# A diffusion step on one core: the order of the modulation's matmuls, the place of two half norms, and the engine of one subtraction

## The chip, the cores and the metric

The kernel runs on one core of a Trainium2 chip. The metric is the device time of one execution in microseconds (us). The core's engines work side by side, each through its own queue in order: TensorE (PE, with PEld for its weight loads), VectorE (DVE), ScalarE (ACT), GpSimd (POOL) and SyncE (SP), which issues most of the DMAs.

## The reference

The reference is one step of a diffusion model with two layers, on 128 context tokens and 512 latent tokens of width 1024 in fp32. Layer 0 mixes the tokens by grouped-query attention (8 query heads, 2 key heads), layer 1 by a gated DeltaNet (8 heads, forward and backward scan). Cut to the part that the change touches:

```python
def modulation(cond, w_mod, b_mod):              # cond: c for latent, c_ctx for context tokens
    m = jax.nn.silu(cond) @ w_mod + b_mod        # (1024) @ (1024, 6 * 1024), once per layer
    return jnp.split(m[..., None, :], N_MOD, axis=-1)

def trunk_layer(x, mods, gain1, gain2, w1, w2, mixer):
    shift1, scale1, gate1, shift2, scale2, gate2 = mods
    mix, aux = mixer(rms_norm(x, gain1) * (1 + scale1) + shift1)
    x = x + gate1 * mix
    h = rms_norm(x, gain2) * (1 + scale2) + shift2
    x = x + gate2 * (jnp.square(jax.nn.relu(h @ w1)) @ w2)     # w1: 1024 x 4096
    return x, aux

def delta_mixer(...):
    ...                                          # projections, convolution, chunked scan per head
    o = rms_norm(o, norm_gain) * silu(z)         # per head of 128
    return o.reshape(B, T, DN_VAL) @ w_out, states
```

After both layers a final RMS norm gives the output.

## The kernel before

**Layout.** Activations lie transposed: 128 features on the partitions, 640 tokens along the row, eight such tiles for the width of 1024. The tokens are worked on in two halves of 320. A product of fp32 precision is made of three matmuls on values split into a high and a low part (high by high, high by low, low by high; `mm3`, line 173 is the matmul). A half tile, that is 128 output features for 320 tokens, takes 24 matmuls of this kind.

**Dense products.** `dense` walks the columns of a weight matrix 128 at a time. `pair` loads the 1024x128 weights into one of three buffers with the tag "raw" (on SP's queue), ScalarE copies the high part, and VectorE, or the engine given as `eng`, subtracts to get the low part (`split`, line 160). Line 160 is also every other elementwise operation of two tensors, line 163 every ScalarE activation, lines 166 and 170 the operations with a scalar on VectorE. In the last product before a norm, five tiles form a group (`last=GROUP`): all their first halves come first, then `mid()` runs the norm of the first half, then the second halves follow. `prefetch` prepares three pairs ahead in six buffers with the tag "wpair".

**Norms.** While a residual is added, `norm_acc` squares each feature tile on ScalarE and adds the squares up on GpSimd. `mod_norm` sums the columns with matmuls of one column (line 289, into "nps"), takes the root on VectorE and PE, and writes the eight modulated tiles, the odd ones with GpSimd's help. It is called once for each half.

**Modulation.** The product with `w_mod` is made in three slabs of 2048 columns for each layer. A slab has eight k-steps, and each of these four matmuls, one for each group of 512 columns. The four write to different 32-row stripes of one PSUM tile, with the conditioning vector, padded to 32 columns, as the stationary operand (line 408). The slabs are fed in different ways. Slab (0, 0) is at the start of the kernel, from buffers of its own. Slab (0, 1) stands beside the key and value projections, and (0, 2) beside the attention's output product, both from two "raw" buffers for each step. Slab (1, 0) stands in the MLP of layer 0, from two "wpair" buffers for each step, tiles named "wm". Slabs (1, 1) and (1, 2) stand in the last three rounds of the DeltaNet, six steps in each, from one "raw" buffer and two activation buffers, fetched one step ahead.

**What sets the order.** Each engine's queue is ordered ahead of time by a planner, which goes by the order in which the program was traced and by when it reckons each instruction to be ready. `weave` traces several pieces of work in turns, by given shares. `pinned` does the same for a main piece and a side piece, and ties each instruction of the side piece on PE, VectorE and ScalarE behind the newest main instruction of the same engine, with an edge that sets order only and no semaphore. In the MLP of layer 0 the main piece has 128 steps (half tiles), and the side piece is slab (1, 0) followed by `presplit`, 58 steps that split the DeltaNet's weights and write them back to memory; the rate is 74 side steps on 128. Near the 123rd half tile `mid2` fetches the first DeltaNet weights and makes the norm of the first half.

**The DeltaNet.** Round r traces the projections of head r, the decay of head r-1, the inverse of head r-2 and the scan of head r-3 together (`delta`). Each scan begins with two loads of a state (line 1151). The rounds 8 to 10 have no projections of heads left; they carry the gates z (`gated`) and slabs (1, 1) and (1, 2). Behind the last round stands `dn_out` of head 7, with norm operations of 128x5, transposes (line 176) and the final scale. `out_begin` makes the first three output tiles, `dense` with `eng=nc.gpsimd` the other five.

Of the kernel before, what the change touches and what calls it, by code (L numbers as in the profile page):

```python
# [37 lines left out]
GROUP = 5  # L38
# [39 lines left out]
def weave(*parts):  # L78
    live = [[0, n, i, g] for i, (g, n) in enumerate(parts)]
    while live:  # L80
        live.sort(key=lambda e: ((e[0] + 1) / e[1], e[2]))
        e = live[0]
        try:
            next(e[3])
            e[0] += 1
        except StopIteration:
            live.pop(0)


PINNED = tuple(getattr(mybir.EngineType, n) for n in ("PE", "DVE", "Activation"))  # L90


def pinned(tc, main, n, side, m):
    nc = tc.nc
    last = {}
    why = mybir.DependencyInfo(mybir.DependencyClass.NoSync, mybir.DependencyReason.DATA)
    traced = lambda i: nc.cur_bb.bb.instructions[i:]
    at = len(traced(0))
    done = step = 0
    for _ in main:  # L100
        step += 1
        for i in traced(at):
            if i.engine in PINNED:
                last[i.engine] = i.name
        at = len(traced(0))
        while done * n < step * m and next(side, True) is None:
            done += 1
            for i in traced(at):
                if i.engine in last:
                    tc.add_manual_dep(i, last[i.engine], why, reason="paced")  # L110
            at = len(traced(0))
    drain(side)


def drain(g):
    for _ in g:
        pass


class Model:  # L120
# [277 lines left out]
    def modulate(self, l, slab, fetch, alloc=None, early=False):  # L398
        nc = self.nc
        acc = alloc or (lambda: self.ps("mod", 1))  # L400
        ps = acc()[:, :512]
        get = lambda k: fetch(self.a["w_mod"][l, k * P : (k + 1) * P, slab * 2048 : (slab + 1) * 2048])
        ahead = get(0) if early else None
        for k in range(FT):
            views = ahead or get(k)
            ahead = get(k + 1) if early and k + 1 < FT else None
            for q in range(4):
                nc.tensor.matmul(  # L408
                    ps[32 * q : 32 * q + 32, :], self.cond[:, k, :], views[q],
                    start=k == 0, stop=k == FT - 1, tile_position=(0, 32 * q),  # L410
                )
            yield
        yield from self.modulation(l, slab, ps, acc)

# [343 lines left out]
    def psum(self, name):  # L758
        return self.tc.tile_pool(name=name, bufs=1, space=bass.MemoryType.PSUM)
# [559 lines left out]
    def run(self):  # L1319
        tc, nc, a = self.tc, self.nc, self.a  # L1320
        pool = lambda name: tc.tile_pool(name=name, bufs=1)
        psum = self.psum
        FC = [f * P for f in range(FT)]
        with pool("start") as self.ph, psum("ps0") as self.pq:
            xs = self.load_x()
            self.setup()
            x = self.transpose_x(xs)
            r0 = self.token_rstd(xs)
            self.columns()
            tail = lambda: max(i for i, t in enumerate(nc.cur_bb.bb.instructions) if t.engine == PINNED[0])  # L1330
            traced = nc.cur_bb.bb.instructions
            after = traced[tail()]
            gm = self.modulate(0, 0, self.fetch_start)
            with tc.issue_after(after):
                for _ in range(FT):
                    next(gm)
            self.key_weights()
            h = self.first_norm(x, r0, gm)
            self.q0 = self.pair(a["attn_w_in"][0], 0, 0)
        with pool("attn") as self.ph:  # L1340
            self.attention(h, x)
            first = self.prefetch(a["attn_w_out"][0], 0, FC)
        with pool("mlp0") as self.ph, psum("ps3") as self.pq:
            self.extra = 3
            x = self.reload(self.xd)
            h = self.new_h()
            nxt = []

            def mid():
                nxt[:] = self.prefetch(a["mlp_w1"][0], 0, FC)  # L1350
                self.mod_norm(x, 0, 1, h, 0)

            weave((self.modulate(0, 2, self.fetch_raw), 18),
                  (self.dense(a["attn_w_out"][0], 0, FC, self.att, self.residual(x, 0, 2), first=first, last=GROUP, mid=mid), 16))
            self.mod_norm(x, 0, 1, h, 1)
            h2 = self.new_h()
            nxt2 = []

            def mid2():
                w = a["dn_w_in"][0]  # L1360
                nxt2[:] = [self.pair(w, 0, kind * D) for kind in (1, 0, 2)]
                self.mod_norm(x, 1, 0, h2, 0)

            def beside():
                yield from self.modulate(1, 0, self.fetch_pairs, early=True)
                yield from self.presplit()

            pinned(tc, self.mlp(0, h, x, nxt, mid2), 128, beside(), 74)
            self.mod_norm(x, 1, 0, h2, 1)
            h = h2  # L1370
            xd = self.spill(x, nc.scalar)
        with pool("delta") as self.ph, psum("ps4") as self.pq:
            self.extra = 0
            self.delta(h, nxt2)
            x = self.reload(xd)
            self.out_begin(x)
        with pool("mlp1") as self.ph, psum("ps5") as self.pq:
            self.extra = 4
            acts = [self.acts[i] for i in range(HEADS)]
            for half in range(2):  # L1380
                for o in range(len(self.first)):
                    self.norm_acc(x, o, half)
            h = self.new_h()
            nxt3 = []

            def mid3():
                nxt3[:] = self.prefetch(a["mlp_w1"][1], 0, FC)
                self.mod_norm(x, 1, 1, h, 0)

            done = len(self.first)  # L1390
            sink = self.residual(x, 1, 2)
            drain(self.dense(a["dn_w_out"][0], 0, FC[done:], acts, lambda o, half, ps: sink(o + done, half, ps), last=GROUP, mid=mid3, eng=nc.gpsimd))
            self.mod_norm(x, 1, 1, h, 1)
            fn = a["final_norm"]
            gain = self.wp.tile([P, D], F32, tag="wpair", bufs=self.NW, name="fgain")
            nc.scalar.dma_start(out=gain, in_=bass.AP(fn.tensor, fn.offset, [[0, P], [1, D]]))

            def final(half):
                cols = self.ps("nps", 2)
                if half == 0:  # L1400
                    blocks = (0, 1)
                    for i, b in enumerate(blocks):
                        self.rstd_cols(cols, i, [(0, P, 0, b * P)])
                else:
                    blocks = (2, 3, 4)
                    self.rstd_cols(cols, 0, [(0, P // 2, 0, 2 * P)])
                    self.rstd_cols(cols, 0, [(P // 2, P // 2, 1, 0)])
                    for i in (1, 2):
                        self.rstd_cols(cols, i, [(0, P, 1, (i + 2) * P - HALF)])
                r = self.finish_rstd(cols[:, : len(blocks)])  # L1410
                for i, b in enumerate(blocks):
                    y = self.wp.tile([P, D], F32, tag="wpair", bufs=self.NW, name=self.nm("y"))
                    for c in range(0, D, 512):
                        ps = self.dense_ps()
                        for j in range(4):
                            self.tr(ps[:, j * P : (j + 1) * P], x[c // P + j][:, b * P : (b + 1) * P])
                        out = y[:, c : c + 512]
                        if c == 0 or b == NBLK - 1:
                            self.stt(out, ps, r[:, i : i + 1], gain[:, c : c + 512], ALU.mult, ALU.mult)
                        else:  # L1420
                            self.act(out, ps, AF.Copy, scale=r[:, i : i + 1])
                            self.tt(out, out, gain[:, c : c + 512], ALU.mult, nc.gpsimd)
                        dst = self.o["y_prompt"][0] if b == 0 else self.o["y_sample"][0, (b - 1) * P : b * P, :]
                        (nc.sync if c else nc.scalar).dma_start(out=dst[:, c : c + 512], in_=out)

            drain(self.mlp(1, h, x, nxt3, lambda: final(0)))
            final(1)


# [39 lines left out]
```

## Time and profile before

| | before |
|---|---|
| time, median of 3 runs (lowest to highest) | 1876.78 us (1871.9 to 1878.34) |
| the profiled execution, its span | 1876.26 us, 1874.5 us |
| busy share PE, PEld, DVE, ACT, POOL | 95%, 88%, 53%, 40%, 16% |
| the chain that ended last | PE 75%, DVE 12%, DMA 6%, ACT 2% |
| DMA | 248.84 MB, mean 133 GB/s |

The span is the time between the first and the last instruction that the profiler saw; the execution's own time is a little longer. A busy share is an average over all stages, so it tells which engine is busiest, not which one a stage waits for. The chain follows the work back from the last instruction, at each step to what released it.

### The profile page before, as it was taken

What the parts mean: (1) busy time and instruction counts of PE and PEld (TensorE: products, weight loads), DVE (VectorE), ACT (ScalarE), POOL (GpSimd) and SP (SyncE); (2) the same over time, 40 slices, a digit from 0 to 9 for tenths busy, and PEclk for the clock granted to TensorE, in tenths of its full rate; (3) what the DMA queues carried; (4) which work ended last, traced back from release to release, by engine and by line L of the source; (5) the groups of instructions that cost most, each with busy time, mean ns of one, the idle gap of its engine ahead of it and who ended that gap; (6) DMA issues with size and microseconds to landing.
All of it is one profiled execution on the core that took longest, in us unless ns stands there. A gap on an engine that the chain in (4) does not pass through costs nothing.

```text
span 1874.5 us, 31001 instructions
## 1 busy us (share of the span) xinstructions
PE 1786.5 (95%) x11971; PEld 1654.7 (88%) x11971; DVE 989.5 (53%) x2301; ACT 757.4 (40%) x1727; POOL 297.7 (16%) x390
## 2 busy tenths in 40 slices
PE   6998999999999999999899999999899999999997
PEld 3777877969999999999898998776699999999997
DVE  5546563724454544556788877443664334343332
ACT  3345552423342423436766565533343223131331
POOL 1143321400010010142021110110251000000012
PEclk8999999999999999999999999999999999999999
DMA  8641136365576676625432333654721222222211
GB/s 322 203 149 35 35 125 205 93 207 178 177 221 194 208 221 189 190 78 175 122 104 83 105 101 112 183 162 139 235 78 57 70 79 74 73 80 71 76 46 57
DMA packets 286761, 248.84 MB, mean 133 GB/s; under 512 B 44591, under 2 KB 246726, under 8 KB 286614
## 3 DMA queue, kind: packets, MB, share of 16 engines
q1 hardware_dynamic: 266768, 207.85, 36.9%
q0 software_dynamic: 9136, 32.18, 4.8%
q10 hardware_dynamic: 10710, 6.83, 1.2%
q8 instruction: 94, 1.54, 0.4%
q14 instruction: 53, 0.43, 0.1%
HBM read 199.00 MB, written 45.20 MB: 130 GB/s over the span
## 4 chain that ended last, share of the span: by engine, by line
PE 75%; DVE 12%; DMA 6%; ACT 2%; issue 2%; POOL 1%; SPq 1%; ACTq 0%; POOLq 0%; DVEq 0%
PE dense L173 33%; PE pd L173 29%; PE scan L173 3%; PE big L173 3%; DVE ptmp L160 2%; PE pd L408 2%; PE mod L408 1%; DMA wide<-gd 1%; DMA raw<-in_w_mod 1%; PE big L176 1%; DVE ptri L1066 1%; DVE cv L166 1%; DMA wm<-in_w_mod 1%; PE S L173 1%; DVE pv L160 1%
## 5 line engine op out<-in xcount | busy, mean ns | idle before, releaser
L173 PE MATMUL pd<-h,w 128*128 128x320 f32 x2016 | 350.6, 319 | 7.8 <-ACT cv L163 3.3
L173 PE MATMUL dense<-a,wx 128*128 128x320 f32 x2238 | 339.7, 311 | 2.4 <-ACT wx L163 1.6
L173 PEld LDWEIGHTS dense<-a,wx 128*128 128x128 f32 x2238 | 332.8, 189 | 5.2 <-ACT wx L163 2.5
L173 PEld LDWEIGHTS pd<-h,w 128*128 128x128 f32 x2016 | 299.0, 189 | 35.1 <-issue 21.8
L163 ACT ACTIVATE wx<-raw 128x1024 fp32r<-128x1024 f32 x132 | 139.8, 1059 | 360.9 <-PE dense L173 217.1
L173 PE MATMUL dense<-h,wx 128*128 128x320 f32 x1776 | 266.8, 309 | 0.0
L173 PEld LDWEIGHTS dense<-h,wx 128*128 128x128 f32 x1776 | 261.6, 188 | 5.9 <-issue 5.0
L160 DVE TENSOR_TENSOR wx<-raw,wx 128x1024 fp32r<-128x1024 f32 x127 | 159.1, 1255 | 156.7 <-ACT wx L163 156.7
L173 PE MATMUL pd<-a,wx 128*128 128x320 f32 x1284 | 194.3, 309 | 0.0
L173 PEld LDWEIGHTS pd<-a,wx 128*128 128x128 f32 x1284 | 189.8, 188 | 0.0
L166 DVE SCALAR_TENSOR_TENSOR x<-dense,c,x 128x192 f32<-128x192 f32 (+2 forms) x147 | 59.7, 434 | 176.0 <-PE dense L173 175.9
L173 PE MATMUL pd<-h,wx 128*128 128x320 f32 x1008 | 151.9, 309 | 0.0
L173 PEld LDWEIGHTS pd<-h,wx 128*128 128x128 f32 x1008 | 148.7, 188 | 1.7 <-DVE a L160 1.7
L160 POOL TENSOR_TENSOR x<-x,half 128x320 f32<-128x320 f32 x48 | 54.1, 1128 | 527.1 <-ACT half L163 526.4
L163 ACT ACTIVATE a<-half 128x320 fp32r<-128x320 f32 x128 | 59.9, 471 | 112.6 <-DVE half L166 112.6
L160 DVE TENSOR_TENSOR a<-half,a 128x320 fp32r<-128x320 f32 x128 | 62.7, 492 | 65.1 <-ACT a L163 65.1
L166 DVE SCALAR_TENSOR_TENSOR x<-pd,c,x 128x128 f32<-128x128 f32 (+2 forms) x87 | 35.8, 440 | 104.9 <-PE pd L173 104.9
L908 POOL DMA_DIRECT2D wd<-w x58 | 30.9, 534 | 369.3 <-ACT w L163 293.2
L166 DVE SCALAR_TENSOR_TENSOR cv<-cv,c,cv 128x644 f32<-128x644 f32 x84 | 78.5, 935 | 17.1 <-ACT cv L163 16.0
L163 ACT ACTIVATE half<-x 128x320 f32<-128x320 f32 x56 | 25.9, 467 | 101.9 <-DVE x L166 101.9
L173 PE MATMUL big<-wide,a 128*128 128x128 f32 x480 | 63.5, 278 | 1.2 <-DMA wide<-td 0.9
L173 PEld LDWEIGHTS big<-wide,a 128*128 128x128 f32 x480 | 58.0, 191 | 7.1 <-ACT a L163 3.1
(289 smaller groups left out, 2486.1 us busy)
## 6 DMA issues: line engine op xcount, KB each, us to landing
raw<-in_mlp_w SPq DMA_DIRECT2D x128, 512.0 KB
wd<-w POOLq DMA_DIRECT2D x58, 512.0 KB, 4.5
w<-wd SPq DMA_DIRECT2D x58, 512.0 KB
raw<-in_w_mod SPq DMA_DIRECT2D x48, 512.0 KB
wm<-in_w_mod SPq DMA_DIRECT2D x32, 512.0 KB
rawp<-in_dn_w_in SPq DMA_DIRECT2D x58, 256.0 KB
a<-in_w_mod SPq DMA_DIRECT2D x32, 256.0 KB
raw<-in_attn_w_in SPq DMA_DIRECT2D x12, 512.0 KB
```

Source lines behind the costliest of these rows:

```text
L160: (eng or self.nc.vector).tensor_tensor(out=out, in0=in0, in1=in1, op=op)
L163: self.nc.scalar.activation(out=out, in_=in_, func=func, **kw)
L166: self.nc.vector.scalar_tensor_tensor(out=out, in0=in0, scalar=s, in1=in1, op0=op0, op1=op1)
L173: self.nc.tensor.matmul(out, l, r, start=first, stop=last)
L176: self.nc.tensor.transpose(out, in_, self.ident[:n, :n])
L408: nc.tensor.matmul(ps[32 * q : 32 * q + 32, :], self.cond[:, k, :], views[q], start=k == 0, stop=k == FT - 1, tile_position=(0, 32 * q),)
L908: self.nc.gpsimd.dma_start(out=d[z], in_=pair[z].bitcast(F32).rearrange("p k c -> p (k c)"))
L1066: nc.vector.tensor_reduce(out=t[:, BASE * i : BASE * i + i], in_=o, axis=AX.X, op=ALU.add)
```

## The change

Three things change.

The four column matmuls of a k-step are traced in the order 3, 2, 1, 0, and each is tied behind the one before with the order-only edge that `pinned` uses. Beside that, slab (1, 0) now takes two side steps for each k-step, and the rate of the side piece is 83 on 128.

The norm of the second half ahead of each MLP is traced after the MLP's first half tile, by `late`.

The last five weight tiles of the DeltaNet's output product have their low parts subtracted on VectorE instead of GpSimd.

```diff
+ORDER = mybir.DependencyInfo(mybir.DependencyClass.NoSync, mybir.DependencyReason.DATA)
+
+def late(g, f):
+    yield next(g)
+    f()
+    yield from g
...
 def modulate(self, l, slab, fetch, alloc=None, early=False):
...
-            for q in range(4):
+            prev = None
+            for q in (3, 2, 1, 0):
                 nc.tensor.matmul(
                     ps[32 * q : 32 * q + 32, :], self.cond[:, k, :], views[q],
                     start=k == 0, stop=k == FT - 1, tile_position=(0, 32 * q),
                 )
+                i = nc.cur_bb.bb.instructions[-1]
+                assert i.engine == PINNED[0]
+                if prev is not None:
+                    self.tc.add_manual_dep(i, prev, ORDER, reason="side by side")
+                prev = i.name
...
-            self.mod_norm(x, 0, 1, h, 1)
             h2 = self.new_h()
...
             def beside():
-                yield from self.modulate(1, 0, self.fetch_pairs, early=True)
+                for _ in self.modulate(1, 0, self.fetch_pairs, early=True):
+                    yield
+                    yield
                 yield from self.presplit()
 
-            pinned(tc, self.mlp(0, h, x, nxt, mid2), 128, beside(), 74)
+            main = late(self.mlp(0, h, x, nxt, mid2), lambda: self.mod_norm(x, 0, 1, h, 1))
+            pinned(tc, main, 128, beside(), 83)
...
-            drain(self.dense(a["dn_w_out"][0], 0, FC[done:], acts, lambda o, half, ps: sink(o + done, half, ps), last=GROUP, mid=mid3, eng=nc.gpsimd))
-            self.mod_norm(x, 1, 1, h, 1)
+            drain(self.dense(a["dn_w_out"][0], 0, FC[done:], acts, lambda o, half, ps: sink(o + done, half, ps), last=GROUP, mid=mid3))
             fn = a["final_norm"]
             gain = self.wp.tile([P, D], F32, tag="wpair", bufs=self.NW, name="fgain")
             nc.scalar.dma_start(out=gain, in_=bass.AP(fn.tensor, fn.offset, [[0, P], [1, D]]))
...
-            drain(self.mlp(1, h, x, nxt3, lambda: final(0)))
+            drain(late(self.mlp(1, h, x, nxt3, lambda: final(0)), lambda: self.mod_norm(x, 1, 1, h, 1)))
             final(1)
```

## Rows read from the trace of the kernel before

**Rows 1.** Windows: length, busy PE, PEld, DVE, ACT, POOL, clock, DMA share, GB/s.

```profile
1169.00:1328.00 159.00, 153.40 (x951) 110.47 (x949) 71.80 (x253) 64.01 (x218) 20.08 (x19) 1.00 0.55 174
```

**Rows 2.** Timeline, last head: start, us, engine, line, operation, [idle before, its releaser].

```profile
1342.97 0.17 DVE L160 TENSOR_TENSOR rst<-rsy 128x5 f32<-128x5 f32 x1
...
1347.82 1.33 PE L176 MATMUL big<-c,a 128*128 128x128 f32 x5 [6.97 <-DVE a L160]
1348.80 3.89 PE L173 MATMUL scan<-a,w 128*128 128x320 f32 x17
```

**Rows 3.** Timeline of PE and ScalarE around the two second-half norms.

```profile
353.02 0.38 PE L289 MATMUL nps<-c,x 128*128 128x1 f32 x2 [2.44 <-POOL x L160]
...
355.26 0.46 ACT L163 ACTIVATE half<-x 128x320 f32<-128x320 f32 x1
...
368.80 7.05 PE L173 MATMUL pd<-h,w 128*128 128x320 f32 x47
...
1401.53 0.38 PE L289 MATMUL nps<-c,x 128*128 128x1 f32 x2 [2.42 <-POOL x L160]
...
1404.23 0.46 ACT L163 ACTIVATE half<-x 128x320 f32<-128x320 f32 x1
...
1415.87 1.33 PE L173 MATMUL pd<-h,w 128*128 128x320 f32 x8
```

**Rows 4.** Chain that ended last, in MLP 0: start, us, what.

```profile
481.08 10.55 PE dense L173 x72
```

**Rows 5.** Timeline of PE in MLP 0.

```profile
378.29 1.05 PE L408 MATMUL mod<-wm,c 128*32 128x512 f32 x4
379.27 2.17 PE L173 MATMUL dense<-h,w 128*128 128x320 f32 x13
381.37 1.05 PE L408 MATMUL mod<-wm,c 128*32 128x512 f32 x4
...
403.12 1.07 PE L408 MATMUL mod<-wm,c 128*32 128x512 f32 x8
```

**Rows 6.** Windows, line 408 alone: length, PE, PEld, clock, DMA share, GB/s.

```profile
60.00:107.00 47.00, 16.83 (x64) 2.31 (x64) 1.00 0.64 204
262.00:330.00 68.00, 12.61 (x64) 2.08 (x64) 0.95 0.68 209
372.00:422.00 50.00, 13.72 (x64) 1.91 (x64) 1.00 0.62 200
1169.00:1328.00 159.00, 40.89 (x128) 5.74 (x128) 1.00 0.55 174
```

**Rows 7.** Waits of PE, 372 to 422: us in all, count, longest.

```profile
PE mod L408 <- DMA wm<-in_w_mod: 1.2, 2, 0.7
```

**Rows 8.** Chain, 1169 to 1328, shares by line.

```profile
by line: PE pd L408 19.0%; PE pd L173 18.5%; PE scan L173 14.3%; PE big L173 10.5%; DMA raw<-in_dn_w_out 6.8%; PE big L176 5.5%; POOL a L160 4.0%; DVE ptmp L160 2.9%; DMA ptmp<-gmd 2.5%; DMA raw<-in_w_mod 2.3%; DVE ptri L1066 1.9%; DVE cv L
```

**Rows 9.** Waits of PE, 1169 to 1328.

```profile
PE big L176 <- POOL a L160: 2.7, 5, 0.8
```

**Rows 10.** Timeline of SP's queue, the state loads of the scans.

```profile
1065.40 0.85 SPq L1151 DMA_DIRECT2D blk<-in_state_delta  x2
1113.57 0.85 SPq L1151 DMA_DIRECT2D blk<-in_state_delta  x2
...
1223.66 1.17 SPq L1151 DMA_DIRECT2D blk<-in_state_delta  x2
...
1285.75 0.86 SPq L1151 DMA_DIRECT2D blk<-in_state_delta  x2
```

**Rows 11.** Waits of PE, 60 to 107.

```profile
PE S L408 <- DMA raw<-in_w_mod: 2.8, 4, 1.5
```

**Rows 12.** Groups by line, 1332 to 1348: busy, mean ns, idle before.

```profile
L160 POOL TENSOR_TENSOR wx<-raw,wx 128x1024 fp32r<-128x1024 f32 x5 | 12.4, 2496 | 42.9 <-ACT wx L163 42.9
...
L170 DVE TENSOR_SCALAR sso<-sso 128x5 f32<-128x5 f32 x1 | 2.4, 2358 | 0.0
```

**Rows 13.** Costliest groups of the whole span.

```profile
L160 DVE TENSOR_TENSOR wx<-raw,wx 128x1024 fp32r<-128x1024 f32 x127 | 159.1, 1255 | 156.7 <-ACT wx L163 156.7
```

More of the change, by code (lines that the diff above doesn't have):

```diff
@@ L95, in pinned @@
     last = {}
-    why = mybir.DependencyInfo(mybir.DependencyClass.NoSync, mybir.DependencyReason.DATA)
     traced = lambda i: nc.cur_bb.bb.instructions[i:]
@@ L109, in pinned @@
                 if i.engine in last:
-                    tc.add_manual_dep(i, last[i.engine], why, reason="paced")
+                    tc.add_manual_dep(i, last[i.engine], ORDER, reason="paced")
             at = len(traced(0))
```

## The prediction

> **What bounds the kernel now.** I read the windows by stage first, then the chain of waits, then the timeline where the change acts. TensorE (PE) is busy nearly everywhere: in the DeltaNet tail from 1169 to 1328 us it shows 153.40 of 159.00 us [rows 1]. So PE time taken away there, or in an MLP, shortens the run, unless another engine's result ends last. The stated exceptions are few and long: one idle stretch of 6.97 us before the last head's transposes [rows 2], and 2.44 and 2.42 us before the second-half norms [rows 3]. All sums are made against the profiled execution's own 1876.26 us, of which the span is 1874.5; the median of the three runs is 1876.78, 0.5 us more.
>
> **Tying the four column groups (modulation).** The matmuls of line 408 stand in runs of two, four, six or eight records; one column group is two records, so a run holds one to four groups. A run of two groups starts at 378.29, the dense product after it at 379.27: 0.98 us. Thirteen dense matmuls then take until 381.37, 2.10 us, where thirteen of a steady stream take 13 x 0.1465 = 1.90 (10.55 us for 72) [rows 4, 5]. So 0.20 us goes to entering and leaving, and a run costs 1.18 us. A run of all four groups, at 403.12, occupies 1.07 us, where the run of two occupies 1.05 [rows 5]: the price is per run, not per group. Dividing the busy time of line 408 by 1.05 gives the runs of each stage [rows 6]: 16 at 60 to 107 us, 12 at 262 to 330, 13 at 372 to 422, 39 at 1169 to 1328. The change asks for 8, 8, 8 and 16. The followers (groups 2, 1, 0) read the earlier loads, so once group 3's load has landed none of them waits. That tied matmuls stay neighbours is borne out by the pairs, which write one PSUM tile and still start together.
>
> [...]
>
> *MLP of layer 0 (372 to 422).* PE alone bounds it: 13 to 8 runs, 5 x 1.18 = 5.9 us. PE also waits 1.2 us there for modulation weights [rows 7]. The new pace asks for one k-step in every second side step: 83 side steps on 128 half tiles is one per 1.54 half tiles of 3.5 us (24 x 0.1465), so a k-step each 10.9 us instead of 128/74 x 3.5 = 6.1. Half of the wait should go, the first steps being bound by when the first weight pair comes free. Term 6.5, ends 5 and 7.1. The pre-splitting that follows starts later (side step 19, half tile 28 instead of 16) and runs denser, with its loads on SP, its writes on GpSimd's queue; it ends at half tile 118 of 128 instead of 116, still ahead of the DeltaNet weights that are fetched at 123. PE has no idle time in between to lose.
>
> *DeltaNet tail (1169 to 1328).* 39 to 16 runs: 23 x 1.18 = 27.1 us of PE time. What of it counts? Line 408 makes up 19.0% of the chain of waits in this stretch, 30.2 us [rows 8], that is about 31 of the 39 runs at 0.98; taken in proportion, 23/39 of 30.2 is 17.8. The rest was filler while a result of VectorE, ScalarE or GpSimd was on its way, and leaves idle time. The five waits for GpSimd, 2.7 us together [rows 9], show that some links have no slack already. Against a latency bound: the scan's state loads, one pair per round, stand 48.2 us apart at 1065.40 and 1113.57, where the round held three projections and no modulation, and 62.1 at 1223.66 to 1285.75 [rows 10]. The chains of a round thus fit in 48 us, and a round of 62.1 less its share of 10 runs (11.8) is 50. Term 18; ends -3 (loads held longer, below) and 27.
>
> *The two raw-fed slabs (60 to 107, 262 to 330).* Ceilings 8 x 1.18 = 9.4 and 4 x 1.18 = 4.7. But their weights pass through three buffers, and a run of four holds two until the second load has landed, so the refill starts later. In the first slab PE already waits 2.8 us for these loads in 4 places [rows 11]: transfers end last there. If all eight steps waited 0.7 more, 5.6 is lost. I take 0 for the first, 2 for the second. Together 2, ends -8 and 14. The start (before 36 us) ends with the last load either way: 0.
>
> **The last head without GpSimd beside it.** While GpSimd subtracts five weight tiles (2496 ns each), VectorE's tiny operations take as long as GpSimd's: the scale of 128x5 takes 2358 ns, its like in a pause of GpSimd 0.17 us [rows 2, 12]. Four such small ones (excess about 2.15 each) and one 128x640 subtraction stand in the chain to the transposes, about 10 us. PE's idle 6.97 us goes, and so does the slow stretch behind it: 17 matmuls from 1348.80 take 3.89 us, against 17 x 0.1465 + 0.16 = 2.65, another 1.24. That is 8.2 at most. The cost: five subtractions now on VectorE, 1255 ns each [rows 13], 6.3 us. They come after the head's chain in program order, so they fall into its gaps, but VectorE runs its queue in order and one that waits for its load holds the chain behind it. The 10 us freed against 8.2 needed leave some 2 for that. If all five stood in the chain, 8.2 - 6.3 = 1.9 is left. Term 7, ends 1.9 and 8.2. The buffers come free earlier too, so the next loads on SP do not move back.
>
> **The norms' second halves.** In layer 0 PE stands from 350.58 to 353.02 for a sum on GpSimd, though the MLP's first tile needs only first-half data, ready before; half 1 starts at 368.80 [rows 3]. These 18.2 us hold 72 dense matmuls (10.55) and 18 small products (2.0 at 0.11): the rest is the wait and a stretch in which matmuls ran slower after it. With the first tile ahead PE goes on at once, but what is late next is the last square on ScalarE, 355.26 + 0.46 = 355.72, held behind a weight conversion; the first tile ends at 350.58 + 3.52 = 354.10. So 1.6 us of idle time stays, the stretch is 10.55 + 2.0 + 1.6 = 14.2, and the gain 4.0. Then the normalised rows: VectorE, ScalarE and GpSimd have less time before half 1 begins and share it with the first tile's ReLU, which costs about 1. Layer 1: 1399.11 to 1415.87 is 16.8; square at 1404.69, first tile done 1402.63, wait 2.1, stretch 14.6, gain 2.1, less 1. Term 4; ends -2 (the clock falls again behind the new waits, and half 1 waits) and 18.2 + 16.8 - 2 x 12.55 = 9.9. GpSimd's and VectorE's norm work moves behind the first tile with PE's; the one DMA that changes place is the final gain on ScalarE's queue, now issued ahead of the norm in program order. It needs a weight buffer that the first tile releases only after half 1, so it must still be queued behind the norm's work.
>
> **Sum.** 18 + 6.5 + 2 + 7 + 4 = 37.5; 1876.3 - 37.5 = 1838.8, forecast 1839.
>
> **Rivals.** *The tail is bound by latency* (0.20): the order of the queues is fixed beforehand, and the removed runs turn into waits; the five waits of [rows 9] speak for it, the round of 48 us against. The tail term is about 0: 1857. *Everything counts* (0.10): 27 + 7 + 9 + 8 + 8 = 59: 1817. *The tie does not keep the groups together* (0.06): the planner puts dense matmuls between them where they become ready one after the other, and the runs stay as many; only the last head and the norms bring 11: 1865. *Held loads, slower* (0.06): a run of four cannot start before its last load, and hands its buffers back together; the 32 k-steps fed through the raw buffers (8 + 8 + 16) each wait on PE. At the longest wait of today, 1.5 us [rows 11], that costs 48 us, 1839 + 48 = 1887. It decides from 37.5/32 = 1.2 us a step. Only the first slab shows such waits of PE now; in the tail, where loads are asked for one step ahead, the chain has one such load, 2.3% or 3.7 us [rows 8].
>
> **Numbers.** The forecast has 0.58. Its own range, from half the doubt in the tail (9) and in the smaller terms (6), is 1824 to 1854. The range for 8 in 10 goes from 1820, short of the ceiling, to 1865, past the latency case, to the untied one. About 0.3%, 6 us, is what a measurement of this kernel can tell from no change. Faster by more: 0.91 (forecast, latency, ceiling, and most of the untied case, less what falls short of it); within: 0.03; slower: 0.06.
>
> **What would show it.** Line 408 in 6 x 8 = 48 runs of about 1.07 us; the tail's busy time on that line near 16 x 1.07 = 17 instead of 40.89; VectorE's 128x5 operations at about 0.17 us and no idle time of 7 us before the last transposes; the first MLP tile starting with no idle time, a wait of 1 to 2 us for a ScalarE square behind it. Wrong would be: idle time of PE in the tail that grows by over 10 us, runs of two on line 408, or VectorE standing for a weight tile ahead of the last head's chain.

## The result and the profile after

The changed kernel took 1863.83 us (median of 4 runs, 1862.01 to 1864.54), against 1875.6 for the kernel before, measured beside it: ratio 0.9942, 95% interval [0.9921, 0.9963]. It is 11.8 us faster, where 37.5 was forecast. The time lies inside the range, but under a third of the gain came, and some of the terms have the wrong sign.

First the page of the profiled execution (1863.72 us), its span and each engine's busy time, share and number of instructions:

```profile
span 1861.9 us, 30985 instructions
PE 1752.3 (94%) x11971; PEld 1657.6 (89%) x11971; DVE 985.3 (53%) x2306; ACT 756.8 (41%) x1727; POOL 287.4 (15%) x385
```

The second line before:

```profile
PE 1786.5 (95%) x11971; PEld 1654.7 (88%) x11971; DVE 989.5 (53%) x2301; ACT 757.4 (40%) x1727; POOL 297.7 (16%) x390
```

PE worked 34 us less than before, and the span is only 12.6 us shorter: most of what PE no longer does has become idle time. To see where, I took the same matmuls in both traces as milestones (the n-th of PE's matmuls in order of time, modulation left out) and compared the times between them, from the first matmul to the last; some 16 us of each span lie outside. The order differs a little where work is interleaved, so a boundary is good to about 1 us; that does not touch the sum. In time, the stage of layer 1's norm comes behind the last head.

```
stage (milestones)                          before   after   gain    forecast term
start                                        41.22   41.06   +0.2       0
attention and its output, two raw slabs     296.61  306.86  -10.3      +2
second-half norm of layer 0                  27.20   26.90   +0.3   \
second-half norm of layer 1                  47.72   50.44   -2.7   /  +4 for both
first part of MLP 0, slab (1, 0)            105.09   99.19   +5.9      +6.5
rest of MLP 0, DeltaNet rounds 0 to 7       675.59  674.15   +1.4       0
DeltaNet's last rounds                      164.31  156.16   +8.2     +18
last head, first output tiles                59.31   49.63   +9.7      +7
output product; MLP 1 to the end            441.41  441.41    0.0       0
```

The mechanism of the ties itself is as forecast. Windows of line 417, which was line 408 (length; busy PE and PEld; clock, DMA share, GB/s), answer to [rows 6]; the first and third stage end later here, since their last steps do:

```profile
60.00:112.00 52.00, 9.39 (x64) 1.30 (x64) 0.92 0.62 196
262.00:332.00 70.00, 8.53 (x64) 1.26 (x64) 0.98 0.61 191
372.00:460.00 88.00, 8.53 (x64) 1.26 (x64) 0.99 0.46 147
1169.00:1328.00 159.00, 17.05 (x128) 2.52 (x128) 0.97 0.59 186
```

The tail's 40.89 us have become 17.05, where 17 was forecast, with all four groups in each run: in MLP 0, for example,

```profile
388.65 1.07 PE L417 MATMUL mod<-wm,c 128*32 128x512 f32 x8
392.33 1.06 PE L417 MATMUL mod<-wm,c 128*32 128x512 f32 x8
```

The PE time went; what it was worth differs from place to place. Waits of PE after (us in all, times, longest), one line each from 56 to 125 us, from 262 to 345 and from 1160 to 1350, against 2.8 in the first [rows 11] and 2.7 in the last [rows 9]:

```profile
PE S L417 <- DMA raw<-in_w_mod: 11.5, 6, 4.1
...
PE mod L417 <- DMA raw<-in_w_mod: 3.9, 7, 0.9
...
PE big L184 <- POOL a L168: 10.4, 6, 5.9
```

The second of them before, from 262 to 335 us:

```profile
PE mod L408 <- DMA raw<-in_w_mod: 1.3, 1, 1.3
```

**The raw-fed slab (0, 1).** The windows from 60 to 112 us, before and then after (length; busy PE, PEld, DVE, ACT, POOL; clock, DMA share, GB/s):

```profile
60.00:112.00 52.00, 47.65 (x292) 31.45 (x293) 19.03 (x67) 13.66 (x29) 10.94 (x8) 1.00 0.63 201
```

```profile
60.00:112.00 52.00, 39.78 (x289) 30.48 (x288) 18.23 (x66) 11.94 (x32) 9.48 (x7) 0.92 0.62 196
```

PE is busy for 7.9 us less and yet gets no further: 289 matmuls in the same 52 us, against 292, and the DMAs move no more than before (196 against 201 GB/s). The last k-step of the slab starts at 106.55 us; before, its last run started at 105.22. So the runs saved here did not bring the slab's end forward, and the timeline shows what came on top (start, us, operation, idle time before it), first a line of before, then after:

```profile
105.22 1.05 PE L408 MATMUL S<-raw,c 128*32 128x512 f32 x4 [1.50 <-DMA raw<-in_w_mod]
```

```profile
101.41 1.07 PE L417 MATMUL S<-raw,c 128*32 128x512 f32 x8 [2.65 <-DMA raw<-in_w_mod]
106.55 1.93 PE L417 MATMUL S<-raw,c 128*32 128x512 f32 x8 [4.08 <-DMA raw<-in_w_mod]
109.23 1.12 PE L184 MATMUL S<-c,x 128*128 128x128 f32 x4 [0.74 <-ACT x L171]
110.00 3.55 PE L181 MATMUL S<-key,x 128*128 128x320 f32 x12
...
117.21 1.92 PE L181 MATMUL S<-key,x 128*128 128x320 f32 x12
```

Within the last of these waits for loads the granted clock falls to 0.5, from 103.88 us on for 10.24 us: the 12 matmuls at 110.00 take 3.55 us, the next 12 like them 1.92.

**The tail.** Timeline of PE before, then of PE and of SP's queue after, around the same work:

```profile
1169.56 1.04 PE L408 MATMUL pd<-raw,c 128*32 128x512 f32 x2
...
1171.17 1.05 PE L408 MATMUL pd<-raw,c 128*32 128x512 f32 x2
...
1176.96 0.77 PE L176 MATMUL big<-c,a 128*128 128x128 f32 x5 [0.83 <-POOL a L160]
```

```profile
1173.23 1.13 PE L181 MATMUL pd<-h,w 128*128 128x320 f32 x6
...
1180.28 1.33 PE L184 MATMUL big<-c,a 128*128 128x128 f32 x5 [5.92 <-POOL a L168]
...
1195.15 0.62 PE L417 MATMUL pd<-a,c 128*32 128x512 f32 x2
```

```profile
1179.50 10.32 SPq L1113 DMA_DIRECT2D wide<-td  x16
1189.86 1.86 SPq L463 DMA_DIRECT2D a<-in_w_mod  x4
```

Before, two runs of slab (1, 1), one group each, stood at 1169.56 and 1171.17, and the wait for GpSimd there was 0.83 us. Now no modulation runs until 1195: the raw loads have landed (SP issued the first three by 831.13), but a tied step also waits for its two loads into activation buffers, which SP issues only at 1189.86, behind sixteen loads of the inverse. PE stands 5.92 us, and the clock is at 0.5 from 1179.07 for 6.83 us.

**The norms.** The wait ahead of the second-half norms is not gone but has another releaser; these lines answer to [rows 3]:

```profile
366.24 0.45 ACT L171 ACTIVATE half<-x 128x320 f32<-128x320 f32 x1
366.74 0.58 PE L297 MATMUL nps<-c,half 128*128 128x1 f32 x2 [2.27 <-ACT half L171]
...
1390.24 0.38 PE L297 MATMUL nps<-c,half 128*128 128x1 f32 x2 [2.68 <-ACT half L171]
```

2.44 and 2.42 us for GpSimd's sum have become 2.27 and 2.68 for ScalarE's square, and the clock falls to 0.5 at 366.70 and at 1390.70, each time for 6.83 us; before, it fell at 354.63 for 6.83 us and at 1402.52 for 3.41.

**The last head.** It went as forecast; these lines answer to [rows 2] and [rows 12]:

```profile
1328.48 0.16 DVE L178 TENSOR_SCALAR sso<-sso 128x5 f32<-128x5 f32 x1
...
1334.78 0.77 PE L184 MATMUL big<-c,a 128*128 128x128 f32 x5 [1.00 <-DVE a L168]
1335.30 2.15 PE L181 MATMUL scan<-a,w 128*128 128x320 f32 x13
```

### The profile page after: what moved, and what is told of

It is laid out like the page before. It is cut to its first block, busy times and chain, and to the rows that moved or that the text cites. A ratio compares the mean times of both kernels' runs of the same rounds, so it can differ in the third digit from the quotient of the medians.

```text
span 1861.9 us, 30985 instructions
## 1 busy us (share of the span) xinstructions
PE 1752.3 (94%) x11971; PEld 1657.6 (89%) x11971; DVE 985.3 (53%) x2306; ACT 756.8 (41%) x1727; POOL 287.4 (15%) x385
## 3 DMA queue, kind: packets, MB, share of 16 engines
q10 hardware_dynamic: 10710, 6.83, 1.2%
## 5 line engine op out<-in xcount | busy, mean ns | idle before, releaser
L168 DVE TENSOR_TENSOR wx<-raw,wx 128x1024 fp32r<-128x1024 f32 x132 | 165.9, 1259 | 157.5 <-ACT wx L171 157.5
```

The costliest lines, as they stand in the source:

```text
L168: (eng or self.nc.vector).tensor_tensor(out=out, in0=in0, in1=in1, op=op)
```

## The experiments

Each kernel was timed beside the kernel before; a gain is the difference of the medians, followed by the ratio with its interval.

**The raw-fed ties alone** (the kernel before, with the ties in slabs (0, 1) and (0, 2) only).

```diff
+            tie = (l, slab) in ((0, 1), (0, 2))
-            for q in range(4):
+            for q in (3, 2, 1, 0) if tie else range(4):
...
+                if tie and prev is not None:
+                    self.tc.add_manual_dep(i, prev, ORDER, reason="side by side")
```

> Only the two slabs that are fed from the raw buffers, (0, 1) and (0, 2), have their four column groups tied (order 3 to 0); all else is as before. Theory 'held loads': a tied step needs both of its loads and gives both buffers back together, so PE waits 8 to 9 us more for modulation weights in slab (0, 1), 3 to 4 us in (0, 2), which is about what the 12 runs saved are worth, and the clock falls behind the waits: about 10 us slower than before, 1884 to 1887. Rival 'the price per run decides, the rest is chance of the clock': the runs saved and the waits cancel, within 3 us of before, 1873 to 1879. Forecast on record: 2 us faster.

Measured: 1887.87 against 1875.11, 12.8 us slower, 1.0072 [1.0057, 1.0086]. PE's wait for these loads is 11.9 us in the first slab, and the stage takes 307.25 us (306.86 in the changed kernel). So the ties are the loss, and the rival falls. That they lose by the buffers that they hold is shown by the run with six buffers, below.

```profile
PE S L419 <- DMA raw<-in_w_mod: 11.9, 6, 4.0
```

**The tail's ties alone** (the same condition with `l == 1 and slab > 0`).

> Only slabs (1, 1) and (1, 2) in the last DeltaNet rounds are tied; all else is as before. Theory 'lost filler': a tied step can't start before its last load, so the first steps move from 1169 to about 1195, PE stands some 5 us more for GpSimd and the clock falls there, so that only 8 to 9 of the 27 us of runs come out: 1866 to 1869. Rival 'bound by latency whatever is tied': 0 to 3 us, 1873 to 1876. Forecast on record: 18 us, 1858.

Measured: 1863.4, 11.7 us faster, 0.9942 [0.9925, 0.9959]. The last rounds take 155.76 us against 164.31, 8.6 less, and PE waits for GpSimd as in the changed kernel. The total is below the expected 1866: in its profiled execution the attention stage, which this edit does not touch, is 3.4 us shorter than in that of the kernel before, with the clock at 0.5 for 5.4 us of it and not 15.1 (last section).

```profile
PE big L185 <- POOL a L169: 10.4, 6, 5.9
PE big L185 <- DVE a L169: 7.6, 1, 7.6
```

**The late norms alone** (`late` around both MLPs, as in the change).

> Only the two second-half norms are moved behind the MLP's first half tile. Theory 'the wait moves, and the clock falls behind it': PE stands 2.3 to 2.7 us for ScalarE's last square instead of 2.4 for GpSimd's sum, runs half a window of matmuls at the lower clock again, and half 1 waits about 1 us: 2 to 4 us slower in all, 1877 to 1880. Rival 'the norm is a gain and the clock's phase in the changed kernel hid it': 4 to 5 us faster, 1871 to 1872. Forecast on record: 4 us faster.

Measured: 1872.61, 2.5 us faster, 0.9991 [0.9978, 1.0004]: neither expectation, no clear difference. PE waits 1.5 and 2.1 us for the square; the stage of the first norm is shorter by 3.9 and the next one longer by 1.0, but that first stage also varies from 24.7 to 27.2 us in kernels whose norm stands where it was.

**The subtraction on VectorE alone** (`eng=nc.gpsimd` dropped).

> Only the five low parts of the DeltaNet's output weights are subtracted on VectorE instead of GpSimd. Theory 'VectorE's small operations were held by GpSimd': the 7 us of idle PE ahead of the last head's transposes shrink to about 1 us, and the slow stretch behind them goes with it: 9 us faster, 1866 to 1868. Rival 'the tail that ended earlier made the room': 2 to 5 us, 1871 to 1874, VectorE's weight tiles standing in the chain. Forecast on record: 7 us faster.

Measured: 1864.11, 11.0 us faster, 0.9944 [0.993, 0.9959]; the last head's stage takes 50.00 us against 59.31. What PE waits for from 1325 to 1350 us, against 6.97 for VectorE [rows 2]:

```profile
PE pd L173 <- ACT x L163: 0.3, 1, 0.3
PE big L176 <- DVE a L160: 0.2, 1, 0.2
```

The theory holds, and the rival of weight tiles in the chain falls: with no tail tied there is room for them too. This part alone is worth nearly the whole gain of the change. The four parts, each alone, measured -12.8, 11.7, 2.5 and 11.0, together 12.4 us; with the 5.9 of MLP 0, which was not run alone, that makes 18.3, and the whole change measured 11.8. The parts do not simply add, and no run shows what the rest is made of.

**The changed kernel without the raw-fed ties** (`tie = fetch != self.fetch_raw`).

> The changed kernel with the ties taken from the two raw-fed slabs (0, 1) and (0, 2), whose groups are traced 0 to 3 again. Theory 'held loads': the 12.8 us that these ties cost alone come back, PE's wait for the loads of slab (0, 1) falls from 11.5 us to about 3, and the clock falls less often behind it: 1850 to 1854. Rival 'the loss came from the other parts or from the clock's phase': less than 4 us come back, 1860 to 1864.

Measured: 1851.22, 24.4 us faster than before, 0.9871 [0.9851, 0.9892], and 12.6 better than the changed kernel. PE's wait for the loads of slab (0, 1) falls to 2.1 us (2.8 before). As expected.

**The same, and the norms ahead of the MLPs again.**

```diff
+            self.mod_norm(x, 0, 1, h, 1)
             h2 = self.new_h()
-            main = late(self.mlp(0, h, x, nxt, mid2), lambda: self.mod_norm(x, 0, 1, h, 1))
+            main = self.mlp(0, h, x, nxt, mid2)
...
+            self.mod_norm(x, 1, 1, h, 1)
-            drain(late(self.mlp(1, h, x, nxt3, lambda: final(0)), lambda: self.mod_norm(x, 1, 1, h, 1)))
+            drain(self.mlp(1, h, x, nxt3, lambda: final(0)))
```

> As the kernel before it in this list, and the two second-half norms stand ahead of the MLPs again as at first. Theory 'the late norms bring nothing, a wait for a square in place of a wait for a sum': within 2 us of that kernel. Rival 'the late norms gain 4 as forecast': 3 to 5 us slower than that kernel.

Measured: 1851.02, 0.2 us from the kernel above it, 0.9875 [0.985, 0.9899]. The late norms bring nothing that can be measured.

**Ties kept, six buffers for slab (0, 1).**

```diff
-            r = self.raw([P, 2, 512])
+            r = self.scr("rawm", 3, [P, 2, 512]) if own and i == 0 else self.raw([P, 2, 512])
```

> The changed kernel, with the first load of each k-step of slab (0, 1) in three buffers of its own, so that the slab's loads have six buffers and not three; the ties stay. Theory 'a tied step holds two of three buffers': loads run ahead, PE's wait for them in slab (0, 1) falls from 11.5 us below 5, and 4 to 7 us come back: 1857 to 1860. Rival 'the loads are bound by the DMA, and any order in which PE reads a step's last load first waits for it': the wait stays over 8 us, 1861 to 1865.

Measured: 1848.11, 27.5 us faster than before, 0.9858 [0.9837, 0.9878], 15.7 better than the changed kernel and more than expected. PE's wait for the loads in the first slab is 1.5 us:

```profile
PE S L417 <- DMA raw<-in_w_mod: 1.5, 3, 0.5
```

So it was the buffers, not the DMA's speed: a tied step takes two of three and gives them back together, so that the next step's second load can't start before it is done. From 60 to 70 us the DMAs move 213 GB/s in the changed kernel and 340 with six buffers (columns as in [rows 1]):

```profile
60.00:70.00 10.00, 8.25 (x62) 6.00 (x61) 5.82 (x37) 2.08 (x11) 0.00 (x0) 1.00 0.64 213
```

```profile
60.00:70.00 10.00, 8.96 (x66) 5.66 (x70) 4.85 (x35) 1.46 (x6) 0.00 (x0) 1.00 0.94 340
```

Six buffers without ties were not run, so what the ties themselves are worth with them is not shown.

**No raw-fed ties, and the first two k-steps of slab (1, 1) free.**

```diff
+            tie = fetch != self.fetch_raw and not (l == 1 and slab == 1 and k < 2)
```

> As the first kernel of this list (no ties in the raw-fed slabs), and the first two k-steps of slab (1, 1) in the DeltaNet's last rounds are untied too. Theory 'lost filler': their first pairs, whose load is there early, stand at 1169 to 1172 again, PE's wait for GpSimd's product near 1180 falls from 5.9 us to about 1, the clock doesn't fall there, and 3 to 5 us are gained on the first kernel of this list: 1847 to 1850. Rival 'the rounds are bound by their chains': within 1.5 us of that kernel.

Measured: 1843.05, 32.6 us faster than before, 0.9829 [0.9806, 0.9853], 8.2 better than with all sixteen steps tied; 3 to 5 was expected. The last rounds take 150.25 us against 158.64. The two runs stand where they stood, and the wait is short (timeline of PE):

```profile
1160.14 1.05 PE L418 MATMUL pd<-raw,c 128*32 128x512 f32 x2
1161.12 0.71 PE L181 MATMUL scan<-yb,wide 128*128 128x128 f32 x4
1161.76 1.04 PE L418 MATMUL pd<-raw,c 128*32 128x512 f32 x2
...
1167.51 0.77 PE L184 MATMUL big<-c,a 128*128 128x128 f32 x5 [0.78 <-POOL a L168]
```

**Both repairs** (six buffers, slab (0, 1) and (0, 2) tied, the first two steps of slab (1, 1) free).

> The changed kernel with both repairs: three more buffers for slab (0, 1), whose ties stay, and no ties in the first two k-steps of slab (1, 1). Theory 'two separate losses, held loads and lost filler': the gains add up, 1863.8 - 15.7 - 8.2 = 1840, 1837 to 1843. Rival 'both give back the same falls of the clock': no better than the better of the two alone, 1843 to 1846.

Measured: 1842.42 (1838.24 to 1845.19), 0.9814 [0.9794, 0.9835]: inside the theory's range, but no better than the kernel above by a clear margin, so it does not by itself show that the gains add up. The last rounds are as short as there (150.75). In its profiled execution the attention stage takes 296.63 us, 7 more than in the next kernel, which differs there only in one weight load near its end.

**The third weight pair behind the squares.**

```diff
-                nxt[:] = self.prefetch(a["mlp_w1"][0], 0, FC)
+                nxt[:] = self.prefetch(a["mlp_w1"][0], 0, FC[:2])
...
+            nxt.append(self.pair(a["mlp_w1"][0], 0, 2 * P))
             h2 = self.new_h()
```

> As the kernel before it in this list, and the third of the weight pairs that are prepared ahead of each MLP is loaded and converted behind the residual's last squares instead of ahead of them. Theory 'the late norm's new wait is a square held behind a weight conversion on ScalarE': PE's wait of 2.3 to 2.7 us behind the first half tile falls below 1 us in both layers, the clock stays up, and 3 to 6 us are gained on the kernel before it in this list: 1834 to 1838. Rival 'the square is late because VectorE and ScalarE are behind, or the third pair is then late': no gain, or up to 3 us slower.

Measured: 1840.05, 0.9812 [0.9795, 0.9828]. The expected drop of the wait below 1 us did not come: in layer 0 it is 1.7 us, in layer 1 2.1 (1.6 and 2.3 in the kernel above).

```profile
PE nps L297 <- ACT half L171: 1.7, 1, 1.7
...
PE nps L297 <- ACT half L171: 2.1, 1, 2.1
```

But the edit did not do what it was meant to. These are VectorE's lines, then ScalarE's, around the last square in layer 0:

```profile
345.62 1.23 DVE L168 TENSOR_TENSOR wx<-raw,wx 128x1024 fp32r<-128x1024 f32 x1 [1.57 <-ACT wx L171]
346.76 0.55 DVE L174 SCALAR_TENSOR_TENSOR x<-pd,c,x 128x320 f32<-128x320 f32 x1
```

```profile
347.08 1.06 ACT L171 ACTIVATE wx<-raw 128x1024 fp32r<-128x1024 f32 x1 [1.49 <-DMA raw<-in_mlp_w]
348.04 0.45 ACT L171 ACTIVATE half<-x 128x320 f32<-128x320 f32 x1
```

On ScalarE a weight conversion, which waited 1.49 us for its load, still stands just ahead of the square, and on VectorE the subtraction of another weight tile stands ahead of the residual's addition that the square reads. In layer 0 the order is that of the kernel above. So the theory is neither confirmed nor refuted by this run.

**All of slab (1, 1) free.**

> As the first kernel of this list, with all eight k-steps of slab (1, 1) untied and only slab (1, 2) tied. Theory 'only the first two steps stood where PE had nothing else': the ties of the other six save runs that count, and without them it is 3 to 6 us slower than the first kernel of this list, 1843 to 1846. Rival 'every tied step of the rounds costs filler': faster than that kernel by 2 us or more.

Measured: 1849.42, 0.9859 [0.9842, 0.9876], 7.0 slower than with only two steps free; the last rounds take 158.75 us. The ties of the other six steps save time that counts, more than expected.

**Both repairs, and slab (0, 2) free as well** (`or (l, slab) == (0, 2)` in the exception).

> As the kernel with both repairs (six buffers for slab (0, 1), the first two k-steps of slab (1, 1) untied, 1842.4 us), and slab (0, 2), beside the attention's output product, untied too. Theory 'three buffers hold a tied step there as well': PE's wait for that slab's loads falls from about 4 to 2 us and its idle time between 262 and 350 us from about 10 to 5, against four or five more runs at 1.18; as the clock falls less often there, 1 to 4 us faster: 1838 to 1841. Rival 'the runs saved there pay for the waits': 1 to 3 us slower, 1843 to 1846.

Measured: 1835.65 (1833.8 to 1841.53) against 1877.23, 41.6 us faster than before, 0.9784 [0.9765, 0.9803], the best of all. That is 6.8 better than with that slab tied; the two intervals overlap a little. The wait for its loads from 262 to 350 us, with the slab tied and then free:

```profile
PE mod L418 <- DMA raw<-in_w_mod: 4.9, 6, 2.8
```

```profile
PE mod L418 <- DMA raw<-in_w_mod: 1.6, 2, 1.5
```

3.3 us less of waiting do not make 6.8; the attention stage as a whole went from 296.63 to 285.43 us in the profiled executions, and the clock stood at 0.5 for 37.0 us of it with the slab tied, for 9.1 with it free.

## Why the prediction was wrong

By stages, 24.8 us of the forecast gain are missing: 12.3 in the raw-fed slabs, 9.8 in the tail, 6.4 in the norms and 0.6 in MLP 0, less 2.7 that the last head gave on top and 1.6 in stages that had no term.

**The raw-fed slabs: forecast +2, measured -10 to -13.** This step failed beyond its own ends (-8 to 14). It priced the held buffers at 0.7 us in each of eight steps and set 9.4 us of saved runs against that. The wait rose by 8.7 us in the first slab (11.5 against 2.8) and 2.6 in the second (3.9 against 1.3), 11.3 in all, and PE's busy time on line 408 fell by 11.5: the saved runs paid for the waits and left nothing. The view that said so was in hand: waits for loads end last there [rows 11], and the next load starts when a buffer comes free. The rest goes with the clock, for which the step had no term: it stood at 0.5 for 37.5 and 35.2 us of this stage in the two kernels with these ties and three buffers, and for 3.4 to 15.1 in the seven kernels without them. By the milestones, 3.2 of the 10.3 us were lost up to 124 us, with the first slab, 4.9 in the unchanged code between the slabs, and 2.1 behind that. Whether the falls between the slabs follow from the waits ahead of them is not shown. The rival "held loads" named this mechanism, but priced it as all or nothing, 32 steps at the longest wait, and so gave it 0.06; in part, in one stage, it should have been a term. With six buffers the loss is gone.

**The tail: forecast 18, measured 8.2** (8.6 alone). The step that failed is "taken in proportion, 23/39 of 30.2". The runs are no random sample of the chain: two of the removed ones stood in a gap that nothing else filled, and a tied step needs its latest load, so it could not stand there. With the first two steps left free the stage takes 150.25 us, a gain of 14, near the forecast. The forecast's own sign of error had come: PE's idle time in this stretch grew from 5.6 us [rows 1] to 18.3 by the window after,

```profile
1169.00:1328.00 159.00, 140.75 (x1008) 118.74 (x1007) 81.83 (x273) 72.54 (x246) 21.17 (x20) 0.97 0.59 186
```

**The norms: forecast 4, measured nothing** (0.2 us between the kernels with and without). The new wait for the square was named, at 1.6 and 2.1 us; it is 2.3 and 2.7. What failed is that the slow stretch behind the old wait was counted as gone. The clock falls behind the new one as well (6.83 us in layer 0 before and after, 3.41 and then 6.83 in layer 1). Run alone, the late norm was followed by no fall in layer 0, and its stage took 23.3 us; three kernels with the norm in its old place and no fall there took 24.7 to 25.0. That is 1.4 us or a little more, and the next stage took 1.0 of it back. The end "the clock falls again", -2, was the right case. That the stage of the norm in layer 1 became 2.7 us longer is not put down to a part: it is 47.7 to 50.5 us across the runs, longest in two kernels of which one has the norm in its old place.

**MLP 0: forecast 6.5, measured 5.9.** Not run alone; in all eight other kernels with slab (1, 0) tied this stage takes 98.0 to 99.5 us, in those without 103.9 to 106.1. Five runs at 1.18 us are 5.9.

**The last head: forecast 7, measured 9.7** (9.3 alone), above the upper end of 8.2: the weight tiles on VectorE fell into gaps at no cost to the chain, and the small operations run at 0.16 us. The upper end counted one idle stretch of 6.97 us; run alone, this part takes PE's idle time in the stage from 8.8 to 0.9 us. The 128x5 scale took 2358 ns beside GpSimd's subtractions of 2496 ns [rows 12], and 0.16 us in the changed kernel, where GpSimd has no instruction from 1328 to 1344 us. By what GpSimd's subtraction lengthened it, no run shows.

**What was not in the sum:** 1.4 us between 475 and 1150 us, where only the pace of the pre-splitting changed. Across the runs this stage takes 673.8 to 677.6 us, so nothing is made of it.

## What to carry to other kernels

Before crediting PE time saved, ask of each stage what ends last there: where PE waits for loads, and these for buffers, the matmuls saved here only lengthened the wait (11.5 us of PE time less, 11.3 us of waiting more in the raw-fed slabs), and a tie that makes a step wait for its latest load holds the buffers longer still. Tying work together takes away its use as filler, so leave untied the steps that stand where PE has nothing else (150.25 against 158.64 us for the last rounds), or give the tied steps buffers for two of them (1.5 us of waiting in slab (0, 1) with six buffers, 11.5 with three). A rival that can act in part belongs in the sum, stage by stage.

## What the runs showed of the hardware

In these runs the same code took different times, at a different granted clock. The first kernel with both repairs and the one with the third weight pair later took 296.63 and 289.37 us for the attention stage. From 112 to 262 us their code is the same; the windows there, in this order:

```profile
112.00:262.00 150.00, 136.89 (x814) 122.22 (x814) 94.85 (x263) 78.98 (x173) 52.13 (x52) 0.93 0.18 54
```

```profile
112.00:262.00 150.00, 135.30 (x845) 118.48 (x844) 98.52 (x267) 80.61 (x177) 52.35 (x52) 0.99 0.19 55
```

PE is busy about as long in both, at a granted clock of 0.93 and 0.99, and gets through 814 and 845 matmuls. Counted by milestones, the same 812 matmuls of this stretch take 149.97 and 144.62 us, with the clock at 0.5 for 20.5 and 3.4 us of them. In the four kernels where the clock did not fall in this stretch at all, these matmuls take 141.1 to 141.3 us; in the changed kernel, with 17.1 us at 0.5, they take 148.4. So two profiled executions of a stage can differ by some 7 us with next to nothing changed, and a part worth less than that is read from its own waits and from several runs, not from one pair of traces.
